# A test of an expert's token count, and its further block, moved between the expert's two products

## The chip, the cores and the metric

The kernel runs on one core of one Trainium2 chip. The metric is device time in microseconds (us), the median of several runs. A difference of about 0.2% (2.2 us) is what a measurement of this kernel can tell from no change.

In the profile, PE is TensorE's matmuls and PEld its weight loads, DVE is VectorE, ACT ScalarE, POOL GpSimd and SP SyncE, whose queue issues the loads of weights. L12 is line 12 of the kernel. A float32 product is counted as two matmuls.

## The reference

One layer of a hybrid model over 256 latent tokens of width 1024 with a context of 256 tokens: a modulated norm, four parallel mixers and an output projection, then a mixture of 32 experts, each token going to its four best, and a final norm. The change lies in the experts alone:

```python
def moe(h, w_router, b_router, w_gu, b_gu, w_down, b_down):
    logits = (h @ w_router + b_router).astype(jnp.float32)
    top_vals, top_idx = lax.top_k(logits, TOP_K)          # 4 of 32
    gates = jax.nn.softmax(top_vals, axis=-1)
    ...
    def expert_block(args):
        xb, e = args
        gu = xb @ w_gu[e] + b_gu[e]                        # (1024) x (1024, 2048)
        gt = jnp.minimum(gu[:, :D_FF], SWIGLU_LIMIT)
        up = jnp.clip(gu[:, D_FF:], -SWIGLU_LIMIT, SWIGLU_LIMIT)
        act = (up + 1) * (gt * jax.nn.sigmoid(SWIGLU_ALPHA * gt))
        return act @ w_down[e] + b_down[e]                 # (1024) x (1024, 1024)
```

All is float32. The weights of one expert are 12 MB, those of all 32 are 384 MB.

## The kernel before

The mixers run first, to about 168 us of the profiled span; then a loop over the 32 experts, written out in full, whose instructions stand on each engine in the order in which the source records them.

**Tokens.** Each expert has room for 64 tokens (CAP). Its tokens are picked from the normed rows by a one-hot product (`pick`, line 930), turned (`turn_rows`, 939) and held in XET. The first product, `gate_up` (lines 961 and 972), multiplies them by the expert's gate and up weights into the banks G0 and G1; `swiglu` makes the activation; `turn_act` (989) turns it into AT; the second product, `down` (961 and 998), multiplies by the down weights; `keep` scales the result, and `scatter_part` (1026) adds it to the output rows, a pair of experts at a time. In iteration e the loop runs down(e - 1), then gate_up(e), then picks and turns the rows of e + 1, then turns the activation of e. Even experts have three scatter parts in that place, odd ones one scatter part and `s_pair` (923).

**The count and the further block.** An expert with more than 64 tokens needs a further block of 32 (`block`, lines 1037 to 1081): it picks up to 32 tokens and runs both products for them, with the same weights, into G0, G1 and bank 0. Whether it runs is known on the chip alone. Each of PE, DVE and ACT reads the count from CNT into a register (`values_load`, line 1109) and branches over the block (line 1114). In before this stands at the head of iteration e, so the block of expert e comes after down(e - 1) and ahead of gate_up(e). In the profiled execution one block runs, that of expert 8. Experts 30 and 31 are tested together by other code, which the change leaves alone.

**Weights.** SP issues one load for each unit of 2 MB: units (e,0) to (e,3) are the gate and up weights of expert e, each two of the eight k steps of gate_up; (e,4) and (e,5) are the down weights. There are nine places in SBUF for units, so a unit goes to the place of the unit nine ahead of it in the order: (e+1,3), (e+1,4), (e+1,5) and (e+2,0) to the four gate and up places of expert e, and (e+2,1), (e+2,2) to its down places. Loads are issued in this order from one queue. A load waits for one count of PE's semaphore: that of the last instruction, in the order of the program, that reads its place.

**A block that isn't taken.** A count of a semaphore has to come out the same on both sides of a branch. On the side without the block, PE waits until its earlier products are done and then adds the block's counts (92) in one go. Whoever waits for a count within the block or after it waits for that place.

The lines that the change touches:

```python
            if e < NE - 2:
                r = nc.values_load(CNT[0:1, e:e + 1], min_val=0, max_val=L, engines=engines)
            if e > 0:
                down(e - 1, mis[1])
                load_to(e * NUN + NPAIR)
            if e < NE - 2:
                with tc.If(r > CAP):
                    block(e, CAP, G0, G1, GH, TH, UP)
```

Of the kernel before, what the change touches and what calls it, by code (L numbers as in the profile page):

```python
# [16 lines left out]
L = 256  # L17
KT = D // P
NE = 32
TOPK = 4  # L20
EPS = 1e-6
CAP = 64
# [47 lines left out]
def tile_hybrid_moe(tc, x, ctx, vec, mats, const, pos_col, pos_row, rows, bias, w_mod, w_in, w_out,  # L70
                    w_gu, w_down, out):
    nc = tc.nc
    pe, dve, act, pool, sp = nc.tensor, nc.vector, nc.scalar, nc.gpsimd, nc.sync

    with tc.tile_pool(name="big", bufs=1) as big, tc.tile_pool(name="acc", bufs=1, space=PSUM) as acc_pool, \
# [7 lines left out]
        CNT = big.tile([1, NE + 1], I32, name="CNT")  # L83
        bank = [acc_pool.tile([P, 512], F32, name=f"bank{i}") for i in range(8)]

        def R(off, n):
            return B[:, off:off + n]
# [498 lines left out]
        def load_to(n):  # L586
            while nxt[0] < min(n, NE * NUN):
                e, u = stream[nxt[0]]
                load_unit(nxt[0], e, u)
                nxt[0] += 1  # L590
# [307 lines left out]
        GH, TH, UP = R(O_GH, 512), R(O_TH, 512), R(O_UP, 512)  # L898
# [7 lines left out]
        G0, G1 = bank[4], bank[5]  # L906
# [8 lines left out]
        def gated(pr):  # L915
            p = PP[pr % 2]
            e0 = 2 * pr
            dve.tensor_tensor(out=PGf.rearrange("p (c e s) -> p c e s", c=2, e=2), in0=p,
                              in1=GT[:, :, e0:e0 + 2].unsqueeze(3).to_broadcast([P, 2, 2, CAP]), op=ALU.mult)
# [13 lines left out]
        def picked():  # L933
            act.activation(XE, mis[0], AF.Copy)  # L934
# [25 lines left out]
        def bias_mm(dst, e, col, g):  # L960
            pe.matmul(dst[64 * g:64 * g + 64, :], E3[:, e:e + 1].to_broadcast([96, CAP]), T[:, col:col + 512],  # L961
                      start=True, stop=False)

        def gate_up(e, xt):
            for b, dst in enumerate((G0, G1)):
                for g in range(2):
                    bias_mm(dst, e, b * 1024 + g * 512, g)
            for k in range(KT):
                w = wt[e, k]
                for b, dst in enumerate((G0, G1)):  # L970
                    for g in range(2):
                        pe.matmul(dst[64 * g:64 * g + 64, :], xt[:, k % 4, (k // 4) * 64:(k // 4) * 64 + 64],  # L972
                                  w[:, b * 1024 + g * 512:b * 1024 + g * 512 + 512], start=False, stop=(k == KT - 1))
# [18 lines left out]
        def down(e, dst, ks=range(KT)):  # L992
            for g in range(2):
                if ks[0] == 0:
                    bias_mm(dst, e, 2048 + g * 512, g)
            for k in ks:
                for g in range(2):
                    pe.matmul(dst[64 * g:64 * g + 64, :], AT[:, k % 4, (k // 4) * 64:(k // 4) * 64 + 64],  # L998
                              dn[e, k, g], start=False, stop=(k == KT - 1))
# [20 lines left out]
        def keep(dst, p0, ps):  # L1020
            for g in range(2):
                dve.tensor_tensor(out=dst[p0:p0 + 64, 512 * g:512 * g + 512], in0=ps[64 * g:64 * g + 64, :],  # L1022
                                  in1=G2B[64 * g:64 * g + 64, :], op=ALU.mult)

        def scatter_part(s, o, c, q, a=0, b=512, last=False):
            pe.matmul(Y[c][q][:, a:b], s[:, c * P:(c + 1) * P], o[:, 512 * q + a:512 * q + b], start=False, stop=last)  # L1026
# [56 lines left out]
        engines = [ENG.PE, ENG.DVE, ENG.Activation]  # L1083
# [21 lines left out]
        parts = [(0, 0), (0, 1), (1, 0), (1, 1)]  # L1105
        for e in range(NE - 1):
            pr, par = divmod(e, 2)
            if e < NE - 2:
                r = nc.values_load(CNT[0:1, e:e + 1], min_val=0, max_val=L, engines=engines)
            if e > 0:  # L1110
                down(e - 1, mis[1])
                load_to(e * NUN + NPAIR)
            if e < NE - 2:
                with tc.If(r > CAP):  # L1114
                    block(e, CAP, G0, G1, GH, TH, UP)
            if e > 0:
                keep(OP[(e - 1) // 2 % 2], 64 * ((e - 1) % 2), mis[1])
            mine = parts if e == NE - 2 else parts[3:] if par else parts[:3]
            adds = [lambda c=c, q=q: scatter_part(SS[(pr - 1) % 2], OP[(pr - 1) % 2], c, q) for c, q in mine]
            adds = adds if pr > 0 else []  # L1120
            gate_up(e, XET)
            if e == NE - 2:
                load_to(NE * NUN)
            pick(PP[(e + 1) // 2 % 2][:, :, (e + 1) % 2, :])

            swiglu()
            picked()
            for f in adds[:1]:
                f()
            turn_rows(XET, mis[1])  # L1130
            turn_act(AT)
            for f in adds[1:]:
                f()
            if par == 1:
                s_pair(PGf, SS[(pr + 1) % 2], G1)
            elif e == 0:
                gated(0)
                s_pair(PGf, SS[0], G1)
            if par == 0 and e + 2 < NE:
                one_hot(pr + 1)  # L1140
                gated(pr + 1)
        e = NE - 1
        more = engines + [ENG.SP]
        r = nc.values_load(CNT[0:1, NE:NE + 1], min_val=0, max_val=L + MORE, engines=more)
# [4 lines left out]
        with tc.If(r > CAP + MORE):  # L1149
            kept = dict(wt), dict(dn)  # L1150
            for e in range(NE):
                base = CAP if e >= NE - 2 else CAP + MORE
                r = nc.values_load(CNT[0:1, e:e + 1], min_val=0, max_val=L, engines=more)
# [12 lines left out]
        e = NE - 1  # L1166
# [142 lines left out]
```

## Time and profile before

| What | Value |
|---|---|
| Median of three runs | 1111.02 us (1110.48 to 1111.2) |
| The profiled execution's own time | 1112.09 us |
| Its span, first to last instruction | 1110.3 us |
| Granted TensorE clock, mean | 0.978 |
| PE busy | 1025.7 us, 92% of the span |
| DVE busy | 305.6 us, 28% |
| ACT busy | 128.5 us, 12% |
| DMA, mean over the span | 401 GB/s, 445.59 MB |
| PE at line 972 (first product) | 457.7 us, 2048 matmuls |
| PE at line 998 (second product) | 222.1 us, 992 matmuls |

A busy time is the time in which an engine's instructions run. The page cuts the span into 40 slices of 27.8 us and gives for each how busy the engines were, the clock that TensorE was granted, and what the DMA moved. A timeline lists an engine's instructions in order, those of one line merged into one row, with the idle time before the row and what ended it.

### The profile page before, as it was taken

To read this page: it belongs to the slowest core of one execution; us is meant where nothing else is said; L and a number is where in the kernel's file an instruction comes from. 1 tells how busy PE (TensorE), PEld (TensorE's weight loads), DVE (VectorE), ACT (ScalarE), POOL (GpSimd) and SP (SyncE) were. 2 spreads that over 40 slices of the span, in tenths; PEclk is the share of its full clock that TensorE was granted. 3 is DMA by queue.
4 is the path that set the end of the run, shared out by engine and by line. 5 is a ranking of instruction groups with operands and counts; after the bars stand their busy time and mean duration, and the time that the engine had idled before them with its cause. 6 is when DMAs were issued, how large, how long until landed. Compare 5 with 4: busy or idle time off the path is not lost. (4 is left out here: it accounts for less than half of the span.)

```text
span 1110.3 us, 11952 instructions
## 1 busy us (share of the span) xinstructions
PE 1025.7 (92%) x4932; PEld 435.8 (39%) x4932; DVE 305.6 (28%) x593; ACT 128.5 (12%) x239; POOL 34.6 (3%) x77
## 2 busy tenths in 40 slices
PE   4999988999999989999999999999989898988896
PEld 2665865333333333333333333333333333323333
DVE  5488742121212222121212121212111212111113
ACT  4133430000000000000000000000000000000002
POOL 4102120000000000000000000000000000000000
PEclk8999998999999989999999999999999999999998
DMA  9997888999999998999999999999999999999992
GB/s 298 375 358 314 338 380 333 403 426 426 426 428 424 426 415 357 428 426 427 426 426 426 425 429 425 427 426 426 429 427 424 427 427 428 424 427 427 427 422 119
DMA packets 42098, 445.59 MB, mean 401 GB/s; under 512 B 4676, under 2 KB 6660, under 8 KB 15240
## 3 DMA queue, kind: packets, MB, share of 16 engines
q1 hardware_dynamic: 41352, 443.43, 95.5%
q8 instruction: 80, 1.31, 0.5%
q0 software_dynamic: 640, 0.63, 0.2%
q14 instruction: 26, 0.21, 0.0%
HBM read 442.41 MB, written 1.05 MB: 399 GB/s over the span
## 5 line engine op out<-in xcount | busy, mean ns | idle before, releaser
L972 PE MATMUL bank<-B 128*64 128x512 f32 x2048 | 457.7, 600 | 19.3 <-DMA B<-in_w_gu_dram 18.9
L972 PEld LDWEIGHTS bank<-B 128*64 128x64 f32 x2048 | 167.3, 138 | 290.8 <-issue 242.1
L998 PE MATMUL bank<-B 128*64 128x512 f32 x992 | 222.1, 600 | 2.8 <-PEq L1149 2.8
L976 DVE TENSOR_SCALAR B<-bank 128x512 f32<-128x512 f32 x32 | 22.1, 692 | 455.7 <-issue 403.3
L998 PEld LDWEIGHTS bank<-B 128*64 128x64 f32 x992 | 70.2, 138 | 135.1 <-issue 129.6
L977 ACT ACTIVATE B<-B 128x512 f32<-128x512 f32 x32 | 20.2, 631 | 754.1 <-DVE B L976 754.1
L1022 DVE TENSOR_TENSOR B<-bank,B 64x512 f32<-64x512 f32 x62 | 42.7, 689 | 212.1 <-PE bank L998 211.4
L1026 PE MATMUL bank<-B 128*128 128x512 f32 x136 | 69.1, 616 | 1.2 <-DVE B L1079 1.1
L930 PE MATMUL bank<-B 128*64 128x512 f32 x256 | 61.5, 592 | 0.9 <-DVE B L866 0.9
L961 PE MATMUL bank<-T,E 96*64 96x512 bf16 x190 | 33.4, 394 | 25.4 <-PEq L1114 20.6
L384 PE MATMUL bank<-B 128*128 128x256 f32 x160 | 37.2, 387 | 0.0
L1026 PEld LDWEIGHTS bank<-B 128*128 128x128 f32 x136 | 22.2, 190 | 36.2 <-issue 23.0
L961 PEld LDWEIGHTS <-E 96*64 96x64 bf16 x190 | 10.5, 106 | 65.3 <-issue 64.6
L930 PEld LDWEIGHTS bank<-B 128*64 128x64 f32 x256 | 20.7, 137 | 35.1 <-issue 33.4
L384 PEld LDWEIGHTS bank<-B 128*128 128x128 f32 x160 | 31.1, 195 | 8.3 <-issue 4.3
L942 DVE TENSOR_TENSOR B<-bank,B 128x512 f32<-128x512 f32 x32 | 22.1, 692 | 30.2 <-PE bank L939 30.2
L939 PEld LDWEIGHTS bank<-B 128*128 128x128 f32 x128 | 19.9, 202 | 17.1 <-ACT B L934 16.8
L990 ACT ACTIVATE B<-bank 128x512 f32<-128x512 f32 x32 | 19.1, 597 | 51.6 <-PE bank L989 51.6
L978 DVE TENSOR_SCALAR B<-bank 128x512 f32<-128x512 f32 x32 | 22.1, 691 | 5.3 <-PE bank L972 5.2
L934 ACT ACTIVATE B<-bank 128x512 f32<-128x512 f32 x32 | 19.1, 597 | 38.1 <-PE bank L930 38.1
L539 DVE SCALAR_TENSOR_TENSOR B<-B 128x256 f32<-128x256 f32 x58 | 23.2, 478 | 0.0
L980 DVE SCALAR_TENSOR_TENSOR B<-B 128x512 f32<-128x512 f32 x32 | 22.1, 692 | 3.3
(302 smaller groups left out, 558.9 us busy)
## 6 DMA issues: line engine op xcount, KB each, us to landing
B<-in_w_gu_dram SPq DMA_DIRECT2D x128, 2048.0 KB, 25.9
B<-in_w_down_dram SPq DMA_DIRECT2D x63, 2048.0 KB, 28.8
B<-in_w_mod_dram SPq DMA_DIRECT2D x16, 1024.0 KB, 6.6
B<-in_w_mod_dram SPq DMA_DIRECT2D x16, 512.0 KB, 10.5
B<-in_w_out_dram SPq DMA_DIRECT2D x4, 1024.0 KB
B<-in_w_in_dram SPq DMA_DIRECT2D x8, 384.0 KB, 6.7
B<-in_w_in_dram SPq DMA_DIRECT2D x8, 256.0 KB, 5.1
B<-in_w_down_dram SPq DMA_DIRECT2D x2, 1024.0 KB
```

The costliest lines, as they stand in the source:

```text
L384: pe.matmul(half(b, t), w, UT[:, k, 256:512], start=(k == 0 and t == 0), stop=(k == KT - 1 and t == 1))
L539: dve.scalar_tensor_tensor(dst, src, w, dst, op0=ALU.mult, op1=ALU.add)
L930: pe.matmul(mis[0][64 * g:64 * g + 64, :], p[:, c, :], H[:, c, 512 * g:512 * g + 512], start=(c == 0), stop=(c == 1))
L942: dve.tensor_tensor(out=d4, in0=ps.rearrange("p (j g s) -> p j g s", j=4, g=2), in1=jg(A2s).unsqueeze(3).to_broadcast([P, 4, 2, CAP]), op= ...
L961: pe.matmul(dst[64 * g:64 * g + 64, :], E3[:, e:e + 1].to_broadcast([96, CAP]), T[:, col:col + 512], start=True, stop=False)
L972: pe.matmul(dst[64 * g:64 * g + 64, :], xt[:, k % 4, (k // 4) * 64:(k // 4) * 64 + 64], w[:, b * 1024 + g * 512:b * 1024 + g * 512 + 512], ...
L976: dve.tensor_scalar(GH, G0, 7.0, 0.5, op0=ALU.min, op1=ALU.mult)
L978: dve.tensor_scalar(UP, G1, 7.0, -7.0, op0=ALU.min, op1=ALU.max)
L980: dve.scalar_tensor_tensor(UP, TH, 1.0, UP, op0=ALU.add, op1=ALU.mult)
L998: pe.matmul(dst[64 * g:64 * g + 64, :], AT[:, k % 4, (k // 4) * 64:(k // 4) * 64 + 64], dn[e, k, g], start=False, stop=(k == KT - 1))
L1022: dve.tensor_tensor(out=dst[p0:p0 + 64, 512 * g:512 * g + 512], in0=ps[64 * g:64 * g + 64, :], in1=G2B[64 * g:64 * g + 64, :], op=ALU.mult)
L1026: pe.matmul(Y[c][q][:, a:b], s[:, c * P:(c + 1) * P], o[:, 512 * q + a:512 * q + b], start=False, stop=last)
```

## The change

The count of expert e > 0 is still read at the head of iteration e, that of expert 0 behind its first product. The branch and the block move from between down(e - 1) and gate_up(e) to the end of iteration e, behind the picked rows, the turned activation and the scatter parts, and so ahead of down(e).

```diff
@@ -1105,20 +1105,20 @@
         parts = [(0, 0), (0, 1), (1, 0), (1, 1)]
         for e in range(NE - 1):
             pr, par = divmod(e, 2)
-            if e < NE - 2:
-                r = nc.values_load(CNT[0:1, e:e + 1], min_val=0, max_val=L, engines=engines)
+            count = lambda: nc.values_load(CNT[0:1, e:e + 1], min_val=0, max_val=L, engines=engines)
+            if 0 < e < NE - 2:
+                r = count()
             if e > 0:
                 down(e - 1, mis[1])
                 load_to(e * NUN + NPAIR)
-            if e < NE - 2:
-                with tc.If(r > CAP):
-                    block(e, CAP, G0, G1, GH, TH, UP)
             if e > 0:
                 keep(OP[(e - 1) // 2 % 2], 64 * ((e - 1) % 2), mis[1])
...
             gate_up(e, XET)
+            if e == 0:
+                r = count()
             if e == NE - 2:
                 load_to(NE * NUN)
             pick(PP[(e + 1) // 2 % 2][:, :, (e + 1) % 2, :])
...
             if par == 0 and e + 2 < NE:
                 one_hot(pr + 1)
                 gated(pr + 1)
+
+            if e < NE - 2:
+                with tc.If(r > CAP):
+                    block(e, CAP, G0, G1, GH, TH, UP)
         e = NE - 1
```

PE before, at the turn from one expert to the next: the tail of an odd iteration, the count, the second product (998), the branch and the head of the block (1042, 1046). L923 is `s_pair`, E and T are the biases' factors.

```order
L923 MATMUL bank_75<-B 128x128 x2
L1109 TENSOR_LOAD CNT
L1109 ISA x2
L961 LDWEIGHTS E_65
L961 MATMUL bank_71<-T,E_65 64x512
L961 LDWEIGHTS E_65
L961 MATMUL bank_71<-T,E_65 64x512
L998 MATMUL bank_71<-B 64x512 x16
L1114 COMPARE_AND_BRANCH
L1042 MATMUL bank_70<-B 32x256 x8
L1046 MATMUL bank_70<-B 128x128 x2
```

PE after, in the tail of an even iteration: the rows of the next expert are picked (930) and turned (939), the activation turned (989), the scatter parts (1026) added, and the branch and the block's head follow.

```order
L930 MATMUL bank_70<-B 64x512 x4
L1026 MATMUL bank_72<-B 128x512
L939 MATMUL bank_71<-B 128x128 x4
L989 MATMUL bank_70<-B 128x128 x4
L1026 MATMUL bank_73<-B 128x512
L1026 MATMUL bank_76<-B 128x512
L1144 COMPARE_AND_BRANCH
L1042 MATMUL bank_70<-B 32x256 x8
```

The branch has moved from behind the second product to ahead of it. PE after, where a block ends: the jump past it, the count of the next expert, the second product, and the first product of the next expert (961, then 972) right behind.

```order
L1026 MATMUL bank_77<-B 128x512
L1144 UNCONDITIONAL_BRANCH x2
L1108 TENSOR_LOAD CNT
L1108 ISA x2
L961 LDWEIGHTS E_65
L961 MATMUL bank_71<-T,E_65 64x512
L961 LDWEIGHTS E_65
L961 MATMUL bank_71<-T,E_65 64x512
L998 MATMUL bank_71<-B 64x512 x16
L961 LDWEIGHTS E_65
L961 MATMUL bank_74<-T,E_65 64x512
```

Between the two products of an expert there is now a branch, and between down(e) and gate_up(e + 1) there is none. On SP's queue, around the loop's start (L571 loads gate and up weights, L581 down weights), only the places of its own jumps differ:

```order
 L581 DMA B<-in_w_down_dram 128x4096 [waits DMAHW2_49,DVE_49]
 L571 DMA B<-in_w_gu_dram 128x4096 [waits DMAHW4_49,DMAHW3_49,PE_49]
-L1114 UNCONDITIONAL_BRANCH
 L571 DMA B<-in_w_gu_dram 128x4096 [waits DMAHW5_49,PE_49]
 L571 DMA B<-in_w_gu_dram 128x4096 [waits DVE_49,PE_49]
+L1144 UNCONDITIONAL_BRANCH
 L571 DMA B<-in_w_gu_dram 128x4096 [waits DMAHW6_49,PE_49]
 L581 DMA B<-in_w_down_dram 128x4096 [waits DMAHW7_49,PE_49]
 L581 DMA B<-in_w_down_dram 128x4096 [waits DMAHW0_49,PE_49]
 L571 DMA B<-in_w_gu_dram 128x4096 [waits DMAHW1_49,PE_49]
```

The loads keep their order, and each still waits for a count of PE. Which count differs for the four places of gate and up weights: their last reader in the order of the program is gate_up(e) before, and the block of expert e after.

## Rows read from the trace of the kernel before

**Rows 1.** Page: span; bandwidth in the span's 40 equal slices.

```profile
span 1110.3 us, 11952 instructions
...
GB/s 298 375 358 314 338 380 333 403 426 426 426 428 424 426 415 357 428 426 427 426 426 426 425 429 425 427 426 426 429 427 424 427 427 428 424 427 427 427 422 119
```

**Rows 2.** Stretches: length, busy PE, PEld, DVE, ACT, POOL; clock, DMA, GB/s.

```profile
200.00:390.00 190.00, 184.07 (x866) 71.81 (x866) 41.33 (x64) 13.87 (x25) 0.00 (x0) 1.00 1.01 426
...
440.00:1080.00 640.00, 602.63 (x2763) 224.21 (x2760) 129.21 (x196) 43.16 (x77) 0.00 (x0) 0.99 1.01 426
```

**Rows 3.** Timeline, TensorE, at the end: start, length, instructions, idle time before.

```profile
1054.32 3.65 PE L972 MATMUL bank<-B 128*64 128x512 f32 x16 [1.24 <-DMA B<-in_w_gu_dram]
```

**Rows 4.** Waits of the load queue: waited for, us in total, times, longest.

```profile
SPq L571 <- PE bank L998: 215.5, 42, 10.7
```

**Rows 5.** Stretches in which the stream is short, and the clock at 172.

```profile
172.00:174.00 2.00, 2.00 (x7) 1.06 (x5) 0.00 (x0) 0.00 (x0) 0.00 (x0) 0.50 1.01 434
...
174.00:180.00 6.00, 6.00 (x29) 3.81 (x27) 0.00 (x0) 0.00 (x0) 0.00 (x0) 0.96 0.67 216
...
196.00:200.00 4.00, 4.00 (x22) 1.27 (x18) 0.00 (x0) 0.00 (x0) 0.00 (x0) 1.00 0.78 250
...
414.00:424.00 10.00, 10.00 (x46) 3.32 (x46) 0.15 (x1) 0.00 (x0) 0.00 (x0) 1.00 0.56 198
```

**Rows 6.** Timeline, load queue, around the loop's start.

```profile
145.37 30.95 SPq L571 DMA_DIRECT2D B<-in_w_gu_dram  x4
```

**Rows 7.** Timeline, TensorE, expert 3.

```profile
254.41 13.93 PE L972 MATMUL bank<-B 128*64 128x512 f32 x64
...
272.35 0.41 PE L961 MATMUL bank<-T,E 96*64 96x512 bf16 x2
```

**Rows 8.** Timeline, TensorE, expert 0.

```profile
166.13 1.95 PE L813 MATMUL bank<-B 128*128 128x128 f32 x16
...
170.21 0.62 PE L961 MATMUL bank<-T,E 96*64 96x512 bf16 x3 [1.45 <-issue]
170.45 15.81 PE L972 MATMUL bank<-B 128*64 128x512 f32 x64
...
191.98 0.64 PE L961 MATMUL bank<-T,E 96*64 96x512 bf16 x2 [0.30 <-issue]
```

**Rows 9.** Three single loads of gate and up weights: issue, time to landing.

```profile
L571 SPq DMA_DIRECT2D B<-in_w_gu_dram x1: 328/328/328, 197.3 to 197.3; - x1
...
DMA to landing us min/median/max: 7.8/7.8/7.8
...
L571 SPq DMA_DIRECT2D B<-in_w_gu_dram x1: 328/328/328, 368.2 to 368.2; - x1
...
DMA to landing us min/median/max: 25.9/25.9/25.9
...
L571 SPq DMA_DIRECT2D B<-in_w_gu_dram x1: 327/327/327, 439.2 to 439.2; - x1
...
DMA to landing us min/median/max: 9.0/9.0/9.0
```

**Rows 10.** Timeline, TensorE, the block and expert 8.

```profile
389.92 1.07 PE L1042 MATMUL bank<-B 128*32 128x256 f32 x16
...
393.11 7.07 PE L1057 MATMUL bank<-B 128*32 128x512 f32 x64 [0.72 <-DVE B L1050]
...
415.57 0.62 PE L961 MATMUL bank<-T,E 96*64 96x512 bf16 x4
416.03 13.90 PE L972 MATMUL bank<-B 128*64 128x512 f32 x64
...
435.30 0.41 PE L961 MATMUL bank<-T,E 96*64 96x512 bf16 x2
...
442.74 0.62 PE L961 MATMUL bank<-T,E 96*64 96x512 bf16 x4 [0.16 <-PEq L1114]
```

**Rows 11.** Waits of TensorE: for its own sequencer at the branch.

```profile
PE bank L961 <- PEq L1114: 20.6, 27, 2.2
```

## The prediction

> **What bounds the kernel now.** I read the page's row of bandwidth first, then stretches of it, then who waits for whom. Of the span of 1110.3 us the experts' loop takes all after about 168 us, and in it the DMA moves 422 to 429 GB/s in nearly every fortieth; the reader is to see two kinds of dents, one in the first 200 us and one in the slices with 415 and 357 [rows 1]. By stretches it is 426 GB/s from 200 to 390 and from 440 to 1080 us, while TensorE is busy 97% of the first and 94% of the second [rows 2]. Both run close to full, but one sets the end: a load of 2 MB (2,097,152 bytes) at 427 GB/s takes 4.9 us, six of them an expert 29.4 us, while the steps of TensorE read below sum to 25.9 to 27.3 us for an expert whose weights are there (14.4 + 4.0 to 5.4 + 7.3 + 0.2). At 1054.32 us TensorE still waits for weights [rows 3], so what comes after moves one to one with the stream. A stop of the stream is never made up for; a stop of TensorE is, by 2 to 3.5 us an expert.
>
> When does the stream stop? A load waits for the slot nine units back, that is for TensorE's products: in the queue's own waits those of line 998 alone stand for 215.5 us [rows 4]. At 174 to 180 us the rate is 216, at 196 to 200 us 250, at 414 to 424 us 198 GB/s [rows 5]. Against 427 these cost 6 x 211/427 = 3.0, 4 x 177/427 = 1.7 and 10 x 229/427 = 5.4 us. Each time TensorE was late and no slot was free. These three places decide.
>
> **The change, part by part.** *Moved: the last reader of expert e's four gate and up slots.* Before, it is the first product itself, which gives slots back one by one, 3.5 us apart (13.93/4). In the changed program the block's products come later in the order, so the loads of units (e+1,3) to (e+2,0) wait for the block or, when it isn't taken, for TensorE's count on the other side of the branch, which now stands after pick, turns and scatter products, just ahead of the second product. All four slots come back there at once: the first 10.5 us plus the work between (4 to 5.4 us) later than now, the last 4 to 5.4 us. The two slots of the second product come back as before.
>
> *At the start.* Now unit (1,3), the last of the four issues that end at 145.37 + 30.95 = 176.32, is issued at 176.0 us [rows 6]. The change takes the count and the branch from ahead of expert 0's first product: the seeds end at 166.13 + 1.95 = 168.08, and in place of a start of the product at 170.45 it starts after its biases (0.42) at 168.5 us. Its 15.81 us there hold two microseconds at a granted clock of 0.50, the lower level of 1.2 GHz, behind a stop of 1.45 us [rows 5, 8]; without the stop I take the 13.93 of expert 3, and keep 15.81 as the other end. It ends at 182.4. From its end to the second product's bias 191.98 - 186.26 = 5.7 us pass, and this holds: 188.1, plus 0.16 for a branch that isn't taken, 188.3 us. So (1,3) is issued 12.3 us later than now, and the stream, which stops at about 175 us as now, restarts that much later. The dent at 196 to 200 us goes, since the loads after it are by then still queued: 12.3 - 1.7 = **10.6 us** lost (12.5 with the half clock). At expert 1 it doesn't lose again: (1,3) lands 7.8 us after its issue, as the load issued at 197.3 did [rows 9], at 196.1, five more units last to 220.6, and a new issue must come 7.8 - 4.9 = 2.9 us ahead, by 217.7; TensorE is at that branch at about 188.3 + 7.3 + 14.4 + 4.0 = 214.0, 2 us later where the clock falls again. Later experts have more, because TensorE gains on the stream.
>
> *At the block.* One block is taken, for expert 8, from 389.92 to 415.57 us [rows 10]: 25.65 us. Now the first product of expert 8 comes after it, so no slot is free for 5.4 us. In the changed kernel the block itself frees the slots as its own first products go, from 3.2 us (393.11 - 389.92) after its start, and this dent goes. But TensorE then comes out of the block with the ring full, and expert 9 must give back a slot *in one piece*. In steps: (8,3) is issued at 368.2 and lands 25.9 us later, at 394.1 [rows 9]; with 10.6 it is 404.7. TensorE, now waiting for it, needs 3.5 for the last quarter: 408.2; up to the second product 435.30 - 429.93 = 5.4 (416.03 + 13.90 for the first): 413.6; block 25.65: 439.3; second product 7.3 (435.30 to 442.74, less the branch): 446.6; expert 9's first product 14.4: 461.0; to its branch 4.0, as expert 3 has from 268.34 to 272.35 [rows 7]: 465.0; branch 0.16 and landing 7.8: unit (10,3) lands at 473.0. Now: the load issued at 439.2, unit (10,1), lands 9.0 later [rows 9], at 448.2, and (10,3) two units on, at 458.0. Difference: **15.0 us**. The 10.6 are in it, so the block's net share is 4.4: a new stop of 9.8 less the old one of 5.4. Expert 10 doesn't add: five units on is 497.5, issue by 494.6, its branch at 465.2 + 7.3 + 14.4 + 5.4 + 0.2 = 492.5.
>
> *Branches.* As many as before. 27 of their waits sum to 20.6 us, the longest 2.2 [rows 11]; with 0.16 for the short and about 2.0 for the long that is nine long ones. The two that lie on the path are those of experts 0 and 9. Each is long with a chance of a third: 2 x 1.9 / 3 = 1.3 us, between 0 and 3.8.
>
> *Moved at no cost:* VectorE's and ScalarE's branches come after their work for the next expert and before the second product ends, so 7 us of products cover them; uncovered they would cost about what TensorE's do, 0.16 to 2.2 us [rows 11], which a phase bound by the stream hides again. The taken block's masks on VectorE stood ready under a second product and now follow VectorE's work for the next expert: between 0 and 0.7 us, the block's other wait for VectorE [rows 10], and I take 0. The queue of SyncE keeps its order of loads; the in-order queue is why one late slot holds up the two loads for the second product behind it.
>
> Sum: 15.0 + 1.3 = 16.3 us on the median of 1111.02: 1127 us. The profiled execution took 1112.09 with a span of 1110.3, 0.1% above the median; a difference of 16 us is the same on either.
>
> One price can be set against a page. The load issued with empty queues at 197.3 us took 7.8 us to land. The Trainium skill (SBUF — State Buffer, The DMA setup-cost knee) has a fixed part of about 2 us and 436 GB/s, which I work out to 6.8 us as an estimate; the sum would be 1.0 us less. The row decides.
>
> **The rivals.** *Both jumps are long.* Nine of 27 are; where both on the path are, the sum is 15.0 + 3.8 = 18.8: 1130 us, 1132 with the half clock at the start. The Trainium skill (Runtime: NRT & Kernel Launch, Instruction fetch mechanics) says that a taken branch whose target isn't already fetched stalls for it; if every jump here were such a one this would be the case, but the rows show two thirds that are not.
>
> *Only the start pays.* If TensorE comes out of the block with a slot to spare, because the steps through expert 9 overlap more than my chain has them, the old dent goes and no new one comes: 10.6 - 5.4 = 5.2, 1116 us. For it: the new stop rests on a chain of seven terms. Against: 9.8 us is more than any of them is likely to be off.
>
> *Every expert pays.* If slots returned late in the steady phase too, 20 experts after the block would each lose some; with 1 us each 1111 + 15 + 20 = 1146. The point from which it decides: return later than 24.5 - 2.9 = 21.6 us after (e,3) lands; I count 3.5 + 5.4 + 2.2 = 11.1. So it speaks against.
>
> *Faster: the loads don't wait for a block that isn't taken.* If the slots came back with the first product's quarters after all, the change would only start expert 0 earlier (2 us, and at full clock) and free slots in the block: the dents of 3.0, 1.7 and 5.4 us shrink or go, at most 10.1: 1101 us, and 1106 with the last one left. The point: the issue of (1,3) at 172, not 188 us. The order of the program speaks against it, no time does.
>
> **How the numbers follow.** Forecast 0.60 (1124 to 1130), both jumps 0.13, only the start 0.12, every expert 0.07, faster 0.06, no change because gains and losses cancel 0.02. The likeliest gives 1127. The range leaves out the third rival, the faster one and no change, 15 in 100: 1116 to 1133. Faster by over 0.2% (2.2 us, about what a measurement here can tell): 0.06; within: 0.02; slower: 0.92.
>
> **What would show it.** Units (1,3) to (2,0) issued together at about 188 us, and a hole in the bandwidth from 175 to 190; four issues together once an expert from then on, right before the second product; no hole at 414 to 424; a hole of about 10 us some 460 us into the span; TensorE waiting for weights within its first products soon after the start, since it keeps gaining 2 to 3.5 us an expert on a stream 10.6 us later; 426 GB/s everywhere else. Four issues still 3.5 us apart would prove the main step wrong; holes after 500 us would point to the third rival.

## The result, and the profile after

The changed kernel took 1138.83 us (median of 3 runs, 1136.05 to 1139.9) against 1111.02: a ratio of 1.0246, 95% interval 1.0217 to 1.0276. It is slower, as forecast, but by 27.8 us and not by 16, and lies above the range of 1116 to 1133. The profiled execution has a span of 1137.0 us, 26.7 more than before.

The first places to look are again the bandwidth in fortieths and stretches of it. The page of the kernel after, span and bandwidth in 40 slices:

```profile
span 1137.0 us, 11949 instructions
...
GB/s 303 382 355 318 359 310 203 427 365 430 428 424 429 425 427 380 249 431 420 421 427 426 427 427 426 427 422 422 428 398 416 425 406 427 429 426 425 425 429 150
```

Five stretches of it (stretch, length, busy PE, PEld, DVE, ACT, POOL with their instructions, clock, DMA share, GB/s), first of the kernel before, then of the kernel after:

```profile
170.00:190.00 20.00, 19.00 (x83) 11.53 (x83) 3.33 (x5) 1.30 (x3) 0.00 (x0) 0.91 0.89 356
190.00:240.00 50.00, 47.37 (x220) 18.10 (x222) 8.82 (x15) 3.00 (x6) 0.00 (x0) 0.97 0.99 413
240.00:400.00 160.00, 153.87 (x762) 59.39 (x758) 35.27 (x56) 12.16 (x22) 0.00 (x0) 1.00 1.01 426
400.00:480.00 80.00, 74.31 (x381) 28.75 (x379) 17.61 (x28) 5.21 (x10) 0.00 (x0) 0.96 0.95 398
480.00:1060.00 580.00, 544.38 (x2491) 202.22 (x2488) 120.61 (x184) 40.07 (x72) 0.00 (x0) 0.99 1.01 427
```

```profile
170.00:190.00 20.00, 16.98 (x82) 6.21 (x80) 5.25 (x9) 2.21 (x4) 0.00 (x0) 0.96 0.29 106
190.00:240.00 50.00, 45.10 (x201) 15.41 (x199) 6.91 (x10) 2.10 (x4) 0.00 (x0) 0.91 1.01 427
240.00:400.00 160.00, 147.88 (x681) 56.73 (x679) 34.06 (x52) 11.77 (x21) 0.00 (x0) 0.98 0.99 416
400.00:480.00 80.00, 73.47 (x424) 27.59 (x422) 17.43 (x30) 5.58 (x11) 0.00 (x0) 0.98 0.84 348
480.00:1060.00 580.00, 530.49 (x2408) 202.97 (x2406) 113.96 (x174) 37.13 (x66) 0.00 (x0) 0.96 1.00 423
```

Each difference of rates, times its length, over 427 GB/s, is time lost by the stream: 250 x 20 / 427 = 11.7 us at the start, of which 14 x 50 / 427 = 1.6 come back; 10 x 160 / 427 = 3.7 up to the block; 50 x 80 / 427 = 9.4 around it; 4 x 580 / 427 = 5.4 after it. The sum is 28.6, and the span grew by 26.7 (a rate is rounded to 1 GB/s, which alone is 1.4 us in the last stretch). So the start is 10.1, the block 9.4, and **9.1 us are lost in stretches where the forecast had nothing**, in dents such as 398, 416 and 406 late in the row of the page. Both kernels move the same bytes, so such losses sum to the growth of the span whatever causes them: they say when the stream stood still, and not who held it up.

At the start the queue of loads does what was forecast. Its timeline in the kernel after (start, length, instructions):

```profile
143.58 44.64 SPq L571 DMA_DIRECT2D B<-in_w_gu_dram  x4
...
190.35 25.65 SPq L571 DMA_DIRECT2D B<-in_w_gu_dram  x4
...
433.18 40.05 SPq L571 DMA_DIRECT2D B<-in_w_gu_dram  x4
```

The first row ends at 188.2, where [rows 6] ended at 176.3; unit (1,3) was to be issued at 188.3. The first of the next row of gate and up loads, with two loads of line 581 between, follows within 2.2 us: the slots came back together. The third row shown ends at 473.2 with unit (10,3), whose issue the forecast had at 465.2, right behind expert 9's branch.

What was not forecast stands in the waits of TensorE and in the groups of its products. Waits of TensorE in the kernel after (waited for: us in total, times, longest):

```profile
PE bank L961 <- PEq L1144: 43.2, 10, 5.9
PE bank L961 <- DVEq L1144: 15.9, 18, 0.9
```

Groups of the page, the products of one expert's steps (busy us, mean ns, idle time before them and its releaser), before and then after:

```profile
L972 PE MATMUL bank<-B 128*64 128x512 f32 x2048 | 457.7, 600 | 19.3 <-DMA B<-in_w_gu_dram 18.9 <-issue 0.3
L998 PE MATMUL bank<-B 128*64 128x512 f32 x992 | 222.1, 600 | 2.8 <-PEq L1149 2.8
L961 PE MATMUL bank<-T,E 96*64 96x512 bf16 x190 | 33.4, 394 | 25.4 <-PEq L1114 20.6 <-issue 1.7 <-DVE B L1022 1.5
```

```profile
L972 PE MATMUL bank<-B 128*64 128x512 f32 x2048 | 448.1, 592 | 0.0
L998 PE MATMUL bank<-B 128*64 128x512 f32 x992 | 244.5, 641 | 7.9 <-issue 5.9
L961 PE MATMUL bank<-T,E 96*64 96x512 bf16 x190 | 37.0, 408 | 61.7 <-PEq L1144 43.2
```

Three readings. The wait for weights, 19.3 us before, is gone: after, TensorE never waits for them, so **it is TensorE's own chain that sets the end**, not the stream. The 20.6 us at the branch [rows 11], all 2.2 or less, have become 43.2 us in 10 stops, eight of them of 3.9 to 5.9 us, and 15.9 in 18 of some 0.9. The second product behind them (line 998) runs at 641 ns in place of 600. In sum TensorE's idle time grew from 1110.3 - 1025.7 = 84.6 to 1137.0 - 1029.6 = 107.4 us: 36.3 at line 961 and 5.1 at line 998, less the 19.3 at line 972. The other 3.9 of the 26.7 are a longer busy time.

A long stop shows where it comes from. Here are the branch instructions of TensorE's sequencer around one jump, ns min/median/max and start, first in the kernel before (expert 4's test, behind the second product of expert 3), then in the kernel after (expert 5's):

```profile
L1114 PEldq COMPARE_BRANCH  x1: 6377/6377/6377, 275.4 to 275.4; - x1
```

```profile
L1144 PEldq COMPARE_BRANCH  x1: 6398/6398/6398, 331.5 to 331.5; - x1
L1144 ACTq COMPARE_BRANCH  x1: 45/45/45, 333.0 to 333.0; - x1
L1144 DVEq COMPARE_BRANCH  x1: 56/56/56, 333.1 to 333.1; - x1
```

And TensorE's products there, before and then after (start, length, idle before):

```profile
272.75 7.09 PE L998 MATMUL bank<-B 128*64 128x512 f32 x32
281.94 0.62 PE L961 MATMUL bank<-T,E 96*64 96x512 bf16 x4 [2.11 <-PEq L1114]
```

```profile
332.60 0.38 PE L923 MATMUL bank<-B 128*128 128x128 f32 x2
338.85 0.64 PE L961 MATMUL bank<-T,E 96*64 96x512 bf16 x2 [5.87 <-PEq L1144]
339.27 8.43 PE L998 MATMUL bank<-B 128*64 128x512 f32 x32
```

And the stretch behind each of the two stops (the clock is the third number from the end):

```profile
280.00:284.00 4.00, 2.06 (x12) 0.99 (x14) 1.26 (x2) 0.00 (x0) 0.00 (x0) 1.00 1.01 426
```

```profile
339.00:343.00 4.00, 4.00 (x14) 1.39 (x14) 0.00 (x0) 0.00 (x0) 0.00 (x0) 0.62 1.00 418
```

The jump takes 6.38 us before and 6.40 after: the same. Before, the sequencer is at it at 275.4, while products queued ahead of it run to 279.84, and 2.11 us stick out. After, it is at the branch at 331.5, and all that is queued are a few transposes, done at 332.98; the stop is 5.87. Then 32 products take 8.43 us, and not the 7.04 of the same step of expert 8 in the kernel before: the granted clock of TensorE is 0.62 from 339 to 343 us, a mix of its two levels of 1.2 and 2.4 GHz, after a stop of nearly six microseconds. Shorter stops close together came before the same: behind 0.76, 1.35 and 0.90 us within expert 0, its second product takes 8.43 us too. One instruction packet (queue q8) lies in the stretch 335.4 to 336.7, within the jump, as one lies at 279.2 to 280.5 in the kernel before. The Trainium skill (Runtime: NRT & Kernel Launch, Instruction fetch mechanics) has a taken branch wait for a fetch when its target isn't already there. These two jumps agree, with one packet each, and give the wait its size, 6.38 and 6.40 us.

Read one by one, the 31 branch rows of TensorE's sequencer even sum to less after the change, 61.7 us for 91.9, and 9 of them last over 2 us, for 18 before. So the jumps didn't become longer; they came out from under queued work. Why the same jump takes 0.3 us at one expert and 6 at another stays open.

The 18 stops of 0.9 us are put down to VectorE's queue. TensorE's own rows at one of them, at expert 9, show something nearer: the read of the next count (line 1108), ns and start, and the product behind it.

```profile
L1108 PEldq TENSOR_LOAD <-CNT x1: 306/306/306, 473.0 to 473.0; - x1
L1108 PEldq FUSED_REGOPS  x1: 151/151/151, 473.4 to 473.4; - x1
```

```profile
473.66 0.41 PE L961 MATMUL bank<-T,E 96*64 96x512 bf16 x2 [0.88 <-DVEq L1144]
```

### The profile page after: what moved, and what is told of

The parts are those of the page before. It is cut to its first block, busy times and chain, and to the rows that moved or that the text cites. A ratio compares the mean times of both kernels' runs of the same rounds, so it can differ in the third digit from the quotient of the medians.

```text
span 1137.0 us, 11949 instructions
## 1 busy us (share of the span) xinstructions
PE 1029.6 (91%) x4932; PEld 437.8 (39%) x4932; DVE 305.5 (27%) x593; ACT 128.3 (11%) x239; POOL 34.9 (3%) x77
## 5 line engine op out<-in xcount | busy, mean ns | idle before, releaser
L972 PE MATMUL bank<-B 128*64 128x512 f32 x2048 | 448.1, 592 | 0.0
L998 PE MATMUL bank<-B 128*64 128x512 f32 x992 | 244.5, 641 | 7.9 <-issue 5.9
L977 ACT ACTIVATE B<-B 128x512 f32<-128x512 f32 x32 | 20.2, 630 | 788.4 <-DVE B L976 788.4
L961 PE MATMUL bank<-T,E 96*64 96x512 bf16 x190 | 37.0, 408 | 61.7 <-PEq L1144 43.2
L930 PE MATMUL bank<-B 128*64 128x512 f32 x256 | 65.4, 607 | 0.9 <-DVE B L866 0.9
L961 PEld LDWEIGHTS <-E 96*64 96x64 bf16 x190 | 12.5, 111 | 95.3 <-issue 94.6
## 6 DMA issues: line engine op xcount, KB each, us to landing
B<-in_w_down_dram SPq DMA_DIRECT2D x63, 2048.0 KB, 18.2
```

Of the source, the lines that this page charges most:

```text
L930: pe.matmul(mis[0][64 * g:64 * g + 64, :], p[:, c, :], H[:, c, 512 * g:512 * g + 512], start=(c == 0), stop=(c == 1))
```

## The experiments

Two theories stood after this. *Slots*: the loads' wait for the branch (the late return of the four gate and up buffers, "the tie") makes the loss. *Branches*: the tests at the new place make TensorE late, whatever the loads do. Differences below are between medians of runs on the same chip, against the kernel before there (1107.98 to 1109.78 us). Stretches are set beside the trace of the kernel before shown above. Executions of that kernel spread from 1106 to 1113 us, so a microsecond or two between two traces says little.

**e1: the changed kernel without the tie.** The block's gate and up product reads the rows H in place of the weights, so no load waits for it.

```diff
-                              wt[e, k][:, 512 * g:512 * g + 512], start=False, stop=(k == KT - 1))
+                              R(O_H, 2048)[:, 512 * g:512 * g + 512], start=False, stop=(k == KT - 1))
```

> The changed kernel, but the block's first product reads the normed rows H in place of expert e's gate and up weights (same instructions, shapes and branches; the few tokens above 64 of expert 8 get other numbers). So no load waits for the branch any more. Theory SLOTS (the 27.8 us come from gate and up slots that return at the branch): back to the kernel before or a little under it, 1101 to 1113 us, loads 3.4 us apart again. Theory BRANCH (the branch costs TensorE more at its new place, whatever the slots): stays above 1125 us, with the same long stops of 4 to 6 us ahead of line 961.

Measured: 1141.46 us, +32.7, ratio 1.0286 (1.024 to 1.0332). The start is whole again, and the waits stay (those of 0.9 us as well, 16.1 us in 18). Stretch 170 to 190, and a wait of TensorE:

```profile
170.00:190.00 20.00, 16.98 (x80) 6.15 (x78) 5.24 (x9) 2.21 (x4) 0.00 (x0) 0.96 0.98 414
```

```profile
PE bank L961 <- PEq L1144: 45.8, 10, 6.0
```

So the tests at the new place are enough for the whole loss. The tie is not needed for it.

**e2: the kernel before with the tie.** Four transposes that read expert e's four buffers stand ahead of its second product; the tests stay where they were.

```diff
             if e > 0:
+                for j in range(4):
+                    pe.transpose(mis[1][:, j * P:(j + 1) * P], wt[e - 1, 2 * j][:, 0:P], ident)
                 down(e - 1, mis[1])
```

> The kernel before, branches where they were, with four 128x128 transposes more ahead of down(e - 1), each of which reads the first 128 columns of one of expert e - 1's gate and up places; their results are overwritten. So the slots return just ahead of the second product, as in the changed kernel, and no branch is moved. SLOTS: (1,3) is issued at about 192.5 instead of 176.0 us, 14 to 15 us of stream lost at the start; at expert 8 the slot returns at 435 instead of 419.7, 15 us late in all; total 1125 to 1129 us. BRANCH: TensorE only gets 0.6 us more work an expert, which the stream hides: 1111 to 1114 us.

Measured: 1139.12 us, +30.4, ratio 1.027 (1.0238 to 1.0302), more than the theory of the slots had. Its stretches:

```profile
170.00:190.00 20.00, 17.95 (x80) 10.92 (x77) 4.82 (x8) 1.83 (x3) 0.00 (x0) 0.93 0.13 57
...
400.00:480.00 80.00, 69.29 (x372) 26.04 (x366) 16.23 (x26) 5.20 (x10) 0.00 (x0) 0.94 0.79 329
```

The loss is all at the start (299 x 20 / 427 = 14.0) and at the block (69 x 80 / 427 = 12.9); after 480 us it runs at the 427 of before. By the order of the program, the block at the old place stands ahead of expert 8's first product, so a return tied to the end of that product waits for the block too; this tie is dearer than that of the changed kernel. Each of the two alone gives about what both give together: the losses overlap. Which of them is worth what had to be taken apart further.

**e3, e8: only expert 0 moved, and all but expert 0.** The place of the test is chosen by e (in e8 `new = e > 0`):

```diff
+            new = e == 0
...
+            if e < NE - 2 and not new:
+                with tc.If(r > CAP):
+                    block(e, CAP, G0, G1, GH, TH, UP)
```

> Only expert 0's count and block moved, all others as in the kernel before. SLOTS: about 11 us of stream lost at the start; at expert 8 the old dent of 5.4 us goes, as the stream is then behind; total about 1117 us (1115 to 1119). BRANCH: one branch is worth at most 2 us, and expert 0 starts earlier: 1109 to 1113 us.

> The kernel after with expert 0's test alone put back to its old place: the start loses nothing then. If the losses add (start, block, jumps one after the other), 1138.8 less the 8 to 10 us that expert 0 alone cost: 1128 to 1131. If TensorE's own chain is the bound, and the loss of the start lies within what it falls behind anyway, 1134 to 1139.

Measured: e3 1118.76 us, +10.0 (ratio 1.0086, 1.0055 to 1.0117, which is 6.1 to 13.0 us). The forecast had 10.6 for the start. The 10.0 aren't the start alone, as the old dent at the block shrinks too: by stretches against the kernel before, 9.9 us are lost to 240 us (108 and 428 GB/s, for 356 and 413), and 3.4 come back around the block (416 for 398). Within its interval e3 bears the 10.6 out. e8 1141.04 us (ratio 1.0277, 1.0244 to 1.031), no less than the changed kernel. But it doesn't take the loss at the start away, it moves it on by one expert. The stretch behind the start:

```profile
190.00:240.00 50.00, 47.01 (x219) 19.08 (x221) 8.03 (x14) 2.48 (x5) 0.00 (x0) 0.97 0.76 311
```

To 190 us the stream loses nothing (386 GB/s, for 356). From 190 to 240 the kernel before has 413, so 102 x 50 / 427 = 11.9 us are lost there, where expert 1's slots now are the first to come back late. So e8 can't say what the loss at the start is worth beside the jumps. e1 can: with no tie at all, the time is no less, so the stream's 10 us lie within what TensorE falls behind anyway.

**e4: the kernel before with the block reading H.** A control for e1, with the tests at the old place.

> Control of the first run: the kernel before with the same substitution in the block (H in place of gate and up weights; the tokens above 64 of expert 8 get other numbers). Both theories: no wait changes, since the weights are there when the block runs: 1110 to 1113 us.

One run gave 1111.02 us: reading H costs nothing by itself that one run could show.

**e5, e6, e9: short jumps.** For every expert but 8, whose body is the only one entered, the body is one operation on VectorE, four transposes and one copy on ScalarE: e5 at the new place without the tie, e6 at the new place with it (the transposes read the four buffers, as in the edit shown), e9 at the old place. In e5 and e9 the transposes read the rows H.

```diff
                 with tc.If(r > CAP):
-                    block(e, CAP, G0, G1, GH, TH, UP)
+                    if e != 8:
+                        ...
+                        for j in range(4):
+                            pe.transpose(mis[0][:, j * P:(j + 1) * P], wt[e, 2 * j][:, 0:P], ident)
+                        act.activation(VAT, mis[0][:, 0:256].rearrange("p (j n) -> p j n", j=4), AF.Copy)
+                    else:
+                        block(e, CAP, G0, G1, GH, TH, UP)
```

> The kernel after without the tie (the further block's first product reads the rows H in place of the weights), and the branch's body made short for every expert but 8: one operation on VectorE, four transposes, one copy on ScalarE in place of the block (only expert 8 has more rows than the main pass covers, so no other body is entered). The counts, the tests and their place stay. If the price is the far jump over the block's code, which nothing covers at the new place, the stops of 4 to 6 us ahead of down's first product go, 0.9 us each is left, and the time is that of the stream of weights again, 1104 to 1113. If the price is the test itself (drain, branch, count), the stops stay and the time is 1130 to 1142. By the theory of the slots alone: 1104 to 1113 too.

> As the run before, but with the tie: the block of expert 8 reads the weights, and the short body of every other expert has four transposes that read its four gate/up buffers, so that these buffers come back at the branch, as in the kernel after, but with no far jump. If the late return of the buffers is enough for the whole loss by itself (as with the four transposes at the old place), 1130 to 1139, with TensorE waiting for weights again. If the far jump is the cause of all that the start does not explain, 1116 to 1122. If the return costs what the prediction put on it, 1127.

> The kernel before with the branch's body made short for every expert but 8 (one operation on VectorE, four transposes of the rows H, one copy on ScalarE in place of the block, never entered), all at the old place. If the far jumps are covered at the old place, by queued products or by waits for weights that come anyway, the time stays: 1106 to 1112. If the kernel before pays for them too, as the 1101 of the short jumps at the new place without the tie may say, 1100 to 1105.

Measured: e5 1100.75 us, -9.0 (ratio 0.9919, 0.9899 to 0.994); e6 1118.7 us, +8.9 (1.0089, 1.0066 to 1.0111); e9 1098.39 us, -9.9 (0.9918, 0.9903 to 0.9933). Two waits of TensorE and the stretch around the block in e6:

```profile
PE bank L972 <- DMA B<-in_w_gu_dram: 37.1, 30, 2.0
PE bank L961 <- DVEq L1144: 24.2, 27, 1.0
```

```profile
400.00:480.00 80.00, 72.76 (x420) 27.22 (x422) 17.44 (x30) 5.59 (x11) 0.00 (x0) 0.98 0.91 380
```

The same stretch of e9, and the branch instructions of its TensorE (ns min/median/max):

```profile
400.00:480.00 80.00, 78.43 (x382) 30.19 (x373) 19.78 (x32) 5.75 (x10) 0.00 (x0) 1.00 1.00 420
```

```profile
L1114 PEldq COMPARE_BRANCH  x31: 70/202/322, 165.6 to 992.5; - x31
```

At the branch no stop is over 1.0 us (1.1 in e5), TensorE waits for weights again (23.4 us in e5), and the stream sets the time. With short jumps, the new place without the tie is 0.9 us from the old place (-9.0 against -9.9), too little to tell from none, and the tie costs 17.9 (8.9 + 9.0). With far jumps the new place costs 32.7 without the tie. And e9 says what the kernel before itself pays for its far jumps: 9.9 us, which I had counted at nothing. By stretches most of it lies in the dents where TensorE was late [rows 5]: 420 GB/s for 356 from 170 to 190 us and for 398 from 400 to 480, 3.0 and 4.1 us.

**e7, e10: the count read early.** In both, each count is read right behind the first product's instructions, ahead of the branch; e7 without the tie, e10 with it.

```diff
-            if 0 < e < NE - 2:
-                r = count()
...
-            if e == 0:
+            if e < NE - 2:
                 r = count()
```

> The kernel after without the tie, and with the count of every expert read behind its first product's instructions, before the branch, in place of behind the branch of the expert before. If the read of the count, exposed at the new place with some 0.7 us of each stop, is a large part of the price, 1120 to 1129. If it is the jump over the block's code alone, 1136 to 1143, and the long stops of 4 to 6 us stay as they are.

> The kernel after, tie and far jumps and all, with only the read of each count moved ahead of the branch, behind the first product's instructions. TensorE's own chain gets some 20 us shorter by the run without the tie, and then is 885 us from the first product of expert 0 to that of expert 30, beside 880 us that the tied stream of weights took with short jumps. If the later of two chains sets the time, 1119 to 1126, with waits for weights coming back. If tie and jumps add, over 1130.

Measured: e7 1122.25 us, +12.5, so 20.2 less than e1: over 28 tests that is 0.7 us each for the read of the next count behind the branch (the load by itself is 0.3 us). That it is TensorE's own read, and no wait for VectorE, shows at expert 9 of e7, where the product starts at 468.51 us and VectorE's count behind the branch comes at 469.2. The stops at the jumps stay, 38.4 us in 11. e10 1130.84 us, +22.5 (ratio 1.0196, 1.0167 to 1.0225): outside the 1119 to 1126 of the later of two chains, and at the lower edge of the over 1130 that stood for losses that add. Added up, e7's 12.5 and the tie's 17.9 would be 30.4. A wait of TensorE says why it is less:

```profile
PE bank L972 <- DMA B<-in_w_gu_dram: 4.9, 5, 1.2
```

Weights are waited for again, but only 4.9 us: it seems that there the stream and TensorE's stops take turns in setting the time, so the losses neither simply add nor simply hide one another. How they share the 22.5 I leave open.

**e12, e13: the bodies out of line.** A short body differs from the real one in more than the distance of the jump, so the last pair leaves the bodies as they are. All thirty are moved behind the rest of the program, in the kernel before (e12) and in the kernel after (e13). A test that isn't met now falls through, and expert 8 alone jumps. This changes two things, the distance and whether the usual path jumps at all; e9, where it jumps but not far, tells them apart.

```diff
+    for f in nc.m.functions:
+        bodies = [b for b in f.blocks if b.name.count("_if_") == 1 and b.name.endswith("_true")][:NE - 2]
+        names = {b.name for b in bodies}
+        f.blocks = [b for b in f.blocks[:-1] if b.name not in names] + bodies + [f.blocks[-1]]
```

> The kernel before with the thirty bodies of the branch moved, as they are, behind the rest of the program, so that a test that isn't met falls through to the instruction behind it, and only expert 8 jumps. Nothing else changes. If the distance of the jump is what the short bodies saved, the time is theirs plus two far jumps at expert 8: 1098 to 1104. If the short bodies saved something else (the counts that the other side of the branch adds for a long body), 1107 to 1112.

> The kernel after, tie and all, with the same move of the bodies behind the rest of the program. If the far jumps are all of its loss that the late return of the buffers is not, 1117 to 1123, as with the short bodies, and against the same move of the kernel before it is slower by the 15.0 that the prediction put on the buffers, give or take 5. If the long body's counts are the price, 1130 to 1140.

Measured: e12 1101.65 us, -6.3, ratio 0.994 (0.992 to 0.9961); e13 1126.19 us, +18.2, ratio 1.0159 (1.0136 to 1.0183). The branch instructions of TensorE in e12 (ns min/median/max), where the kernel before has a median of 2394 and a longest of 6435:

```profile
L1114 PEldq COMPARE_BRANCH  x31: 64/64/6316, 165.7 to 998.1; - x31
```

The distance is the cause: a test that falls through takes 64 ns, one that jumps over a short body 202 (e9, 322 at most), one that jumps over the real body up to 6435, and of the 80 instruction packets of the kernel before, 35 are not fetched. **e12 is faster than both kernels**: the same instructions as before, some of them placed elsewhere. By the medians it stands 3.6 us behind e9, though the two intervals overlap. The place where it loses against e9 is expert 8, whose body now lies far: from 400 to 480 us it has 392 GB/s for e9's 420, and its products there run longer (9.72 us in place of the 7.07 of [rows 10]).

e13 was outside its 1117 to 1123, and the 24.5 us against e12 are outside 15 give or take 5. Stretches of e13:

```profile
400.00:480.00 80.00, 67.39 (x374) 24.48 (x374) 17.43 (x30) 5.58 (x11) 0.00 (x0) 0.89 0.80 328
480.00:1060.00 580.00, 532.72 (x2472) 190.59 (x2468) 118.27 (x181) 39.22 (x70) 0.00 (x0) 1.00 1.01 428
```

428 GB/s from 480 us on: without far jumps nothing is lost there. The start is as in the kernel after (109 GB/s from 170 to 190 us, for 106), and the rest is at the block, where the tie makes the stream wait for TensorE and TensorE waits for the far body. Against e6, with 380 in that stretch, this is 52 x 80 / 427 = 9.7 us, and e13 is 9.3 us above e6 (18.2 and 8.9). Its products there:

```profile
401.25 3.65 PE L972 MATMUL bank<-B 128*64 128x512 f32 x16 [1.24 <-DMA B<-in_w_gu_dram]
...
415.84 1.93 PE L1042 MATMUL bank<-B 128*32 128x256 f32 x16 [5.49 <-DVE B L1037]
```

The 5.49 us ahead of the body are put down to VectorE's masks (line 1037) inside it. VectorE's branch and its first instruction in the body:

```profile
L1144 DVEq COMPARE_BRANCH  x1: 67/67/67, 410.0 to 410.0; - x1
```

```profile
415.47 0.22 DVE L1037 TENSOR_TENSOR B<-B 128x64 f32<-128x64 f32 x1 [5.08 <-issue]
```

TensorE's own jump to the body takes 6.29 us from 407.4 and is over at 413.7, so VectorE comes last. Its work ahead of the branch ended at 410.39, and then 5.08 us pass that its branch row of 0.07 doesn't show. In the kernel after, with the body in its place, the same masks hold TensorE up for 0.32 us. So a far jump costs VectorE some 5 us as well, but as a gap behind the row. Then the products of line 1057 take 9.84 in place of 7.07 us, at a granted clock of 0.71 from 420 to 430 us.

**e11: expert 0 tested in the tail.** No count and no branch stands ahead of expert 0's first product, and none is moved; its further block would load its weights again.

```diff
-            if e < NE - 2:
+            if 0 < e < NE - 2:
...
-                base = CAP if e >= NE - 2 else CAP + MORE
+                base = CAP if e == 0 or e >= NE - 2 else CAP + MORE
```

> The kernel before with expert 0 tested in the tail with experts 30 and 31 (its further block would then load its weights again), so that no count and no branch stand ahead of the first product of expert 0, and none is moved. The gap of 1.45 us there goes, and the later branches stay where they are covered: 1106 to 1111. If the start is bound by the loads, within 0.2% of the kernel before.

Measured: 1107.52 us, ratio 0.9992 (0.9978 to 1.0007): no difference that can be told from none. So taking away the stop of 1.45 us of [rows 8] gains nothing. The expectation had this for a start that the loads bind. Whether that is the reason stays open: in its trace the start is shorter by 3.9 us of stream (404 and 427 GB/s to 190 and 240 us, for 356 and 413), and the median doesn't show it.

## Why the prediction was wrong, point by point

*Slower, as forecast.* In part luck. The mechanism that forecast it, the late slots, isn't what sets the time of the changed kernel: e1, without it, is as slow. With short jumps the late slots alone make it slower too, 8.9 us above the kernel before (e6).

*The stream bounds the kernel before.* Right in the long stretches: from 480 us on it has 427 GB/s, and e9 and e12, without far jumps, have 427 and 428, while TensorE waits longer for weights (29.1 us in 28 waits, 30.2 in 33, for 18.9). In the dents it was TensorE, as the prediction itself said, and there its jumps had a price (e9). And "a stop of TensorE is made up for, by 2 to 3.5 us an expert" was used as if it had no end. The 19.3 us at line 972 were all there was to give, and the stops took more than that. In the kernel after TensorE never waits for weights, so the sign that it would soon after the start didn't come, and the sentence is no longer true at any expert.

*The slots come back together at the branch.* Right, by the load queue's rows and by the four issues at once.

*The start, 10.6 us.* Right as a loss of the stream: 10.1 by the stretches, 9.9 in the trace of e3, where expert 0 alone is moved.

*Expert 1 and later experts don't lose again.* Right as far as the slots go: e13 has 429 GB/s from 190 to 240 us, 428 from there to 400 and 428 after the block. In the kernel after they do lose, 9.1 us outside start and block, for the other reason below.

*The block, net 4.4 us.* Wrong in size: 9.4. In e6, with near bodies, it is (398 - 380) x 80 / 427 = 3.4, so the term was about right for a TensorE that isn't late. In the kernel after, the first link of the chain had failed when it began. It let TensorE end expert 8's first product at 408.2, as it then waits for weights; in e13, without far jumps up to there, that product does end at 404.9, after a wait for weights. In the kernel after it ended at some 416.7, as TensorE was late by itself. Its row there:

```profile
403.20 13.47 PE L972 MATMUL bank<-B 128*64 128x512 f32 x61
```

The dent at 414 to 424 us did go (425 GB/s), and the hole near 460 did come (38 from 462 to 474), as forecast. With the bodies near (e6 against e9) the change as a whole is worth 18.8 us, with expert 8's far and no far jump elsewhere (e13 against e12) 24.5, against a forecast of 15.0.

***Branches, 1.3 us.*** **This is the step that failed.** "As many as before", priced with the stops of [rows 11], took what was left of a jump at the old place for the price of a jump. The price stood in the sequencer's own row, 6.38 us, most of it under the second product's queued work. So three things were missing. The same jump loses its cover at the new place (a stop of 5.9 us for one of 2.1). The read of the next count, which stood under a product too, comes out with 0.7 us an expert (20.2 us between e1 and e7). And behind such a stop the products ran at a lower granted clock (8.43 for 7.04 us). Moreover, I let only the two branches count that lie where the stream is late; there are 28, and together they made TensorE the bound.

*VectorE's and ScalarE's branches at no cost.* Right for the jumps over the body: 45 and 56 ns in the rows above; the stops of 0.9 us that are put down to VectorE's queue were TensorE's own read of the count where I looked. VectorE's masks at the block held TensorE up for 0.32 us, within the 0 to 0.7.

*The rivals.* "Both jumps are long" had the long jumps, and left them at two places and at the covered price. "Every expert pays" has the shape that came, holes after 500 us, but not its condition: the slots are not late there without the jumps (e13). The Trainium skill (Runtime: NRT & Kernel Launch, Instruction fetch mechanics) has a taken branch wait when its target must be fetched first. That rule, which the prediction set aside because two thirds of the stops are short, agrees with these traces: some short stops were covered jumps, such as those of 4.41 us at 196.3 and 3.80 at 222.2 in the kernel before, which left 0.16 each. It is not that every jump waits, since the median of the kernel after is 338 ns.

## What to carry to other kernels

Price a branch of TensorE by its row in the sequencer, not by the stop that is left behind it (on VectorE, look at the gap behind the row, too): what is queued ahead of it covers it, and moving it to a place where the engine's queue has run dry uncovers the same jump. Where a bound has slack, add up what all the moved stops take from it before calling them free; the sum here passed 19.3 us and another engine became the bound. And a body that is rarely entered was better placed behind the program, so that the usual path falls through: this alone is worth 0.6% here.

## What the runs showed of the hardware

A test that isn't met costs TensorE 0.06 us when it falls through, 0.2 when it jumps over a short body, and up to 6.4 us when it jumps over the block, at either place; a third to two thirds of the jumps over the block took over 2 us. VectorE's and ScalarE's rows have 0.05 us for it. The far jumps of VectorE into a body behind the program left gaps of 5.70 (e12) and 5.08 us (e13) behind branch rows of 0.07. After the stop of 5.87 us the granted clock was 0.62 for 4 us; after the one of 2.11 it was 1.00. And what a cause is worth depends on the other: far jumps at the new place cost 41.7 us without the tie (32.7 + 9.0, e1 against e5) and 18.9 with it (27.8 - 8.9, the kernel after against e6), as each hides in the waits that the other one makes.
